# S5's small matmuls and the sums of squares with left operands of 64 columns, and S5's gate placed later among the output projection

## The chip, the cores and the metric

The kernel runs on one core of one Trainium2 chip. The metric is the time of one execution on the device, in microseconds (us); lower is better. The core has a matrix engine (PE; its weight loads are shown as a row of their own, PEld), a vector engine (DVE), an activation engine (ACT), a general engine (POOL), and a queue engine (SP) which here issues nearly all transfers between the chip's main memory and the on-chip memory. The engines run side by side. Each works through its own list of instructions in the order in which the program gives them, and an instruction waits until what it needs has been produced. So a matmul late in PE's list never overtakes one that waits ahead of it.

A matmul on PE has a left operand, which is loaded into the array first (LDWEIGHTS, the PEld row), and a right operand that is streamed through it. A float32 operand takes two passes: one matmul in the source is then two LDWEIGHTS and two MATMUL in the trace. Operands of the type F32R take one.

## The reference

Two decoder layers over 512 positions of width 1024. Layer 0 mixes by two paths whose outputs are concatenated and projected; layer 1 mixes by a short convolution. Each layer ends with a gated feed-forward network (FFN). The part that the change touches is layer 0's S5 path, and the normalisations' sums of squares.

```
y = rmsnorm(h, mix_norm_g[0])
p = y @ ev_w_in                                  # 256 columns for S5, 1536 for gMLP
# S5: 16 groups of 16 channels, each drives 64 complex states
x_re, x_im = u @ bb_re, u @ bb_im
h_re, h_im = associative_scan(a, x)              # h[t] = a * h[t-1] + x[t]
a_out = gelu(h_re @ c_re - h_im @ c_im + d_skip * u)
a_out = a_out * sigmoid(a_out @ w_glu + b_glu)   # the gate (GLU)
# gMLP: gelu, rmsnorm of v, 128x128 causal mixing of positions, 6 heads
b_out = u * gate
h = h + concat(a_out, b_out) @ ev_w_out          # the output projection
h = h + conv_ffn(rmsnorm(h, ...))
...
return rmsnorm(h, final_norm_g)
```

## The kernel before, in words

Channels lie on the 128 partitions, the 512 positions along a row, so the residual `h` is eight tiles of 128x512. Every large matmul is done in three F32R matmuls (`mms`, lines 135 to 137): high part by high part, low part by high part, high part by low part. A step's weight is loaded into a `raw` tile, split into a high part `whi` by ACT (line 111) and a low part `wlo` by DVE (line 112); each of these has three buffers, so a load waits until the split three steps earlier is done, and a split waits until the matmuls three steps earlier have read their weights.

The program is a list of steps, one per weight tile. In layer 0 they are: eight steps `eva` of the input projection (`first`), four `evv` (`v_unit`, the second half of gMLP's v), five `evu` (`head`, gMLP's u; the last three also do the mixing `spatial`, whose outputs are the tiles `ab0` to `ab5`), eight `evo` (the output projection of gMLP's part, one of eight output tiles `pe` each), and two `evos` (the output projection of S5's part, four output tiles `pes` each). For the first three `evo` steps the last two of the six inner tiles are put off until all three have done the first four. After `evos` each finished tile of `h` is prepared for the FFN (`xprep`: high part `xhf` on ACT, low part `xlf` on DVE, squares on ACT and POOL), and the FFN's matmuls (`pf`) follow.

S5 is not a step. It is a Python generator, `s5_all`, that writes its instructions between the steps: it yields an estimated cost in us after each piece, and ahead of each step `bg` lets it go on for as many us as a table gives (`BG_A` for the `eva` steps, `BG_B` from there on; its last entry holds for all later steps). Its pieces, in order:

- parameters, and tables of powers, on DVE;
- `s5_near` (line 619): the near part of the kernel, 16 matmuls into `pnr`, an addition on POOL, two transposes into `pnt`, then a way through main memory (`dnr`) into the tile `tm`;
- `s5_state`: matmuls into `pbu`, a scan on DVE, and four tiles `xo` (two for each c, the real and the imaginary part);
- `s5_out` (line 650): for each of two halves i, 8 groups of three matmuls into `py`, then a gelu into `yt`, and a way through main memory: one store into `dy` and eight loads into `yg`, all on the SP queue;
- `s5_glu` (line 668): for each half i two matmuls of 512 columns into `pgl` (one with `yg0`, one with `yg1`), sigmoid on ACT into `sg`, a product on DVE into `so`, and the split into `as0` and `as1`, which the `evos` steps read.

The matmuls into `pbu` already have left operands of 64 columns, and write the upper and the lower 64 partitions in turn:

```
r = slice(64 * (g % 2), 64 * (g % 2) + 64)
PE.matmul(pv[c][r, j * NC:(j + 1) * NC], lhsT=win[c][:, j, r], rhs=us[:, g, :],
          start=True, stop=True)
```

`sum_mm` (line 196) adds the squares over the partitions: a matmul with the squares as left operand and two columns as right operand, per 128 positions. It is used three times: once for the first normalisation (into `pstm`) and twice for the last (into `pstfin`, once per half of the positions). The other normalisations use `wide_stats` instead.

The code fixes which instructions exist and their order of need. Their place in each engine's list is then decided when the program is built: a scheduler that simulates the engines orders them, so pieces of neighbouring steps can be interleaved.

Of the kernel before, what the change touches and what calls it, by code (L numbers as in the profile page):

```python
# [16 lines left out]
P = 128  # L17
# [6 lines left out]
LAG = (2, 3)  # L24
LATE = 2
SP0 = 3
BG_A = (0.0, 2.0, 2.0, 3.0, 4.0, 4.5, 4.5, 4.5)
BG_B = (1.5, 3.0, 3.0, 3.0, 3.4, 3.4, 3.0, 2.5, 2.5, 2.5)
L = 8
NC = T // L  # L30
# [21 lines left out]
def trunk(ctx: ExitStack, tc: tile.TileContext, x, pra, prb, eva, evu, evv, evo, evos, bmat, bmatz, cmat, wglu,  # L52
          wst, bs, odi, odo, up, dn, out):
    nc = tc.nc
    V, G, S, PE = nc.vector, nc.gpsimd, nc.scalar, nc.tensor
# [8 lines left out]
    def pt(name):  # L64
        return ps.tile([P, T], F32, tag="mm", name=name)

    def gt(name, dt=F32R):
        return gp.tile([P, T], dt, tag="g", name=name)
# [10 lines left out]
    onesd = cp.tile([P, 2], F32, name="onesd")  # L79
# [35 lines left out]
    def advance(upto, bg=None):  # L115
        while state["load"] < min(upto + 3, len(steps)):
            load(state["load"])
            state["load"] += 1
        while state["split"] < min(upto + 2, len(steps)):
            split(state["split"])  # L120
            state["split"] += 1

    def run_steps(n0, n1, bg=None, cost=None):

        for i in range(n0, n1):
            advance(i)
            if bg is not None:
                bg(cost(i - n0))
            steps[i][1](*state["spl"][i])
# [65 lines left out]

    def sum_mm(pst, a, n, first, last):
        for i in range(n):
            PE.matmul(pst[:, 2 * i:2 * i + 2], lhsT=a[:, i * P:(i + 1) * P], rhs=onesd,
                      start=first and i == 0, stop=last and i == n - 1)

    def inv_rms(pst, tag, n):
        m = cp.tile([P, 8], F32, tag="m", name=f"m{tag}", bufs=2)[:, :n]
# [43 lines left out]
    env = {}  # L246
# [3 lines left out]
    def bychunk(ap):  # L250

        return ap.rearrange("p (c s) -> p s c", s=L)

    def cvw(ap):
        return ap.rearrange("p (s c) -> p s c", s=L)
# [31 lines left out]
    us = sp.tile([P, NG, NC], F32, name="us")  # L287
# [53 lines left out]
    def head_out(n, pu):  # L341
        ug = sp.tile([P, T], F32, tag="ug", name=f"ug{n}", bufs=SP0 + 1)
        V.tensor_tensor(out=ug, in0=pu, in1=env["rs"], op=ALU.mult)
        S.activation(ug, ug, AF.Gelu_apprx_tanh)
        ugs[n] = ug

    def head(n):
        def f(hi, lo):
            pu = pt(f"phu{n}")
            mms(pu, hi, lo, xs, range(KD), 0, KD - 1)  # L350
            head_out(n, pu)
            if n >= SP0:
                spatial(n - SP0)
            if n == 5:
                for m in range(6 - SP0, 6):
                    spatial(m)
# [19 lines left out]
    bmz = sp.tile([P, 2, 8, 32], F32, name="bmz")  # L376
# [6 lines left out]
    def ttt(o, a, b, op):  # L383
        V.tensor_tensor(out=o, in0=a, in1=b, op=op)  # L384
# [41 lines left out]
    ca = [sp.tile([P, 8, L + 1, 16], F32, name=f"ca{c}") for c in range(2)]  # L426
    win = [sp.tile([P, 8, P], F32, name=f"win{c}") for c in range(2)]
    tm = sp.tile([P, NG, P], F32, name="tm")
# [192 lines left out]
    def s5_near():  # L621

        dd = gt("dd", F32)[:16, :256].rearrange("p (g r) -> p g r", r=16)
        G.tensor_tensor(out=dd, in0=ident[0:16, 0:16].unsqueeze(1).to_broadcast([16, NG, 16]),
                        in1=pa[0:16, A_D:A_D + NG].unsqueeze(2).to_broadcast([16, NG, 16]), op=ALU.mult)
        nr = gt("nr", F32)[:, :256]
        pn = pt("pnr")
        for j in range(8):
            for c in range(2):
                PE.matmul(pn[:, 32 * j:32 * j + 32], lhsT=ca[c][:, j, 0:L, :].rearrange("p n r -> p (n r)"),  # L630
                          rhs=bmz[:, c, j, :], start=(c == 0), stop=(c == 1))
        S.copy(nr, pn[:, :256])
        o = nr[0:16, :].rearrange("p (g r) -> p g r", r=16)
        G.tensor_tensor(out=o, in0=o, in1=dd, op=ALU.add)
        pn2 = pt("pnt")
        for i in range(2):
            PE.transpose(pn2[:, i * P:(i + 1) * P], nr[:, i * P:(i + 1) * P], ident)
        nt = gt("nt", F32)[:, :256]
        S.copy(nt, pn2[:, :256])
        for i in range(2):  # L640
            nc.sync.dma_start(dnr[i * P:(i + 1) * P, :], nt[:, i * P:(i + 1) * P])
        for q in range(L):
            w = 16 * (q + 1)
            nc.sync.dma_start(tm[16 * q:16 * q + 16, :, P - w:],
                              dnr.rearrange("(g h) c -> h g c", h=16)[:, :, :w])
        wgl.append(gt("wglu", F32).rearrange("p (k c) -> p k c", c=256))
        nc.sync.dma_start(wgl[0], wglu)
        yield 1.0

    def s5_out():  # L650
        for i in range(2):
            yg[i] = gt(f"yg{i}", F32)
            py = pt(f"py{i}")
            for g in range(8):
                o = py[:, g * NC:(g + 1) * NC]
                for c in range(2):
                    PE.matmul(o, lhsT=ca[c][:, 4 * i + g // 2, 1:, :].rearrange("p n r -> p (n r)"),
                              rhs=env[f"xo{c}"][i][:, g * NC:(g + 1) * NC], start=(c == 0), stop=False)
                PE.matmul(o, lhsT=tm[:, 8 * i + g, :], rhs=us[:, 8 * i + g, :], start=False, stop=True)
            yt = gt(f"yt{i}", F32)  # L660
            S.activation(yt, py, AF.Gelu_apprx_tanh)
            nc.sync.dma_start(dy[i], yt)
            for g in range(8):
                nc.sync.dma_start(cvw(yg[i][16 * g:16 * g + 16, :]),
                                  dy[i].rearrange("(s h) (g c) -> g h s c", h=16, c=NC)[g])
        yield 2.0

    def s5_glu():
        for i in range(2):
            pgl = pt(f"pgl{i}")  # L670
            for k in range(2):
                PE.matmul(pgl, lhsT=wgl[0][:, k, i * P:(i + 1) * P], rhs=yg[k], start=(k == 0), stop=(k == 1))
            sg = sp.tile([P, T], F32, tag="vsq", name=f"sg{i}")
            S.activation(sg, pgl, AF.Sigmoid, bias=pa[:, A_BG + i:A_BG + i + 1])
            so = sp.tile([P, T], F32, tag="sc", name=f"so{i}", bufs=2)
            ttt(bychunk(so), cvw(sg), cvw(yg[i]), ALU.mult)
            yk[i] = split_to(so, f"as{i}")
            yield 2.0

    def s5_all():  # L680
        yield from s5_params()
        yield from s5_in_w()
        yield from s5_c()
        yield from s5_in_w_turn()
        yield from s5_out_w()
        yield from s5_near()
        yield from rot_table()
        yield from s5_state()
        yield from s5_out()
        yield from s5_glu()  # L690

    class Bg:
        def __init__(self, gen):
# [194 lines left out]
    eA = len(steps)  # L888
    steps += [((evv[kk], 768), v_unit(kk)) for kk in range(4)]
    steps += [((evu[n], 1024), head(n + 1)) for n in range(5)]  # L890
    e1 = len(steps)
    ev = out_group(yk, 2, KD, lambda d, p: add_back(d, p, None), "e", 3, LATE)
    steps += [((evo[d], 768), ev(d)) for d in range(KD)]
    e15 = len(steps)
# [15 lines left out]
    bg = Bg(s5_all())  # L910
# [26 lines left out]
    for k in range(KD):  # L937
        advance(k)
        for q in (2 * k + 2, 2 * k + 3):
            if q < KD:  # L940
                take_x(q)
        bg(BG_A[k])
        first(k, *state["spl"][k])
# [8 lines left out]
    for n in range(6):  # L952
        G.affine_select(out=wt[:, n, :], in_=wt[:, n, :], pattern=[[1, P]], compare_op=ALU.is_ge,
                        fill=0.0, base=0, channel_multiplier=-1)
    run_steps(eA, e15, bg, lambda i: BG_B[min(i, len(BG_B) - 1)])
    bg(1e9)
    run_steps(e15, e2)
    p1.close()
    fp["p"] = ctx.enter_context(tc.tile_pool(name="fp", bufs=2))
# [92 lines left out]
```

## Time and profile before

| | us |
|---|---|
| median of 3 runs | 1074.59 |
| lowest and highest | 1073.94, 1075.92 |
| the profiled execution's own time | 1073.31 |
| its span, first to last instruction | 1071.5 |
| PE busy in that span | 1053.0 |
| DVE, ACT, POOL busy | 670.8, 420.4, 135.4 |

The profile is one execution. In a timeline row the first number is the start in us from the beginning of the span, the second the length of the row's work; x64 at the end means 64 instructions merged in that row. Matmuls are pipelined: a MATMUL of 390 ns is followed by the next one after some 230 ns, so what a matmul costs is the distance from start to start, not its own length. A note in brackets at the end of a row is the idle time of that engine just ahead of it and what ended it. The granted TensorE clock is full (1.00) in all the stretches used here.

### The profile page before, as it was taken

How to read it: one execution, taken by the hardware profiler on the slowest of the kernel's cores; microseconds unless marked ns; L12 is line 12 of the kernel's file. 1: busy time of each engine (PE TensorE's matmuls, PEld its weight loads, DVE VectorE, ACT ScalarE, POOL GpSimd, SP SyncE). 2: the span in 40 equal slices, each digit the busy share in tenths (PEclk: the TensorE clock that was granted, in tenths of full speed). 3: DMA queues.
4: the chain of work that ended last, by engine and by line, in shares of the span. 5: the costliest groups of instructions: out<-in, count | busy, mean ns of one | idle time of the engine just before them, and what ended most of it. 6: DMA issues, size and time to landing. Idle time of an engine off the chain costs nothing.

```text
span 1071.5 us, 12604 instructions
## 1 busy us (share of the span) xinstructions
PE 1053.0 (98%) x4928; PEld 882.3 (82%) x4928; DVE 670.8 (63%) x937; ACT 420.4 (39%) x565; POOL 135.4 (13%) x121
## 2 busy tenths in 40 slices
PE   7999999999999999999999999999999999999996
PEld 6998788888888888888888888888888888888885
DVE  7968369866346663566585564678645664666544
ACT  6444245544134431344522232444423432444343
POOL 3010012201000100011311110302000100010012
PEclk9999999999999999999999999999999999999998
DMA  7451232323323333222323331423232233232322
GB/s 257 128 134 60 89 114 83 100 97 98 99 98 98 98 99 98 99 79 79 120 97 98 98 98 59 138 80 101 76 119 98 89 89 118 98 99 84 84 70 79
DMA packets 39979, 107.17 MB, mean 100 GB/s; under 512 B 10224, under 2 KB 11248, under 8 KB 39920
## 3 DMA queue, kind: packets, MB, share of 16 engines
q1 hardware_dynamic: 39920, 106.37, 31.5%
q8 instruction: 38, 0.62, 0.2%
q14 instruction: 21, 0.17, 0.1%
HBM read 103.08 MB, written 3.28 MB: 99 GB/s over the span
## 4 chain that ended last, share of the span: by engine, by line
PE 98%; DVE 1%; DMA 0%; ACT 0%; issue 0%; SPq 0%; POOL 0%; DVEq 0%; ACTq 0%; POOLq 0%
PE pf L137 15%; PE pf L136 15%; PE pf L135 15%; PE pd L137 11%; PE pd L136 11%; PE pd L135 11%; PE po L137 1%; PE po L135 1%; PE po L136 1%; PE pv L279 1%; PE pv L281 1%; PE pv L280 1%; PE pe L135 1%; PE pe L137 1%; PE pe L136 1%; PE phu L135 1%
## 5 line engine op out<-in xcount | busy, mean ns | idle before, releaser
L111 ACT CAST whi<-raw 128x1024 fp32r<-128x1024 f32 (+3 forms) x204 | 198.7, 977 | 450.0 <-PE pd L136 200.7
L112 DVE TENSOR_TENSOR wlo<-raw,whi 128x1024 fp32r<-128x1024 f32 (+3 forms) x204 | 246.7, 1210 | 49.7 <-ACT whi L111 49.2
L137 PE MATMUL pf<-xhf,wlo 128*128 128x512 f32 x704 | 273.9, 389 | 0.0
L136 PE MATMUL pf<-xlf,whi 128*128 128x512 f32 x704 | 273.6, 389 | 0.0
L135 PE MATMUL pf<-xhf,whi 128*128 128x512 f32 x704 | 273.5, 389 | 0.0
L136 PEld LDWEIGHTS pf<-xlf,whi 128*128 128x128 f32 x704 | 132.1, 188 | 27.8 <-DVE xlf L145 0.2
L135 PEld LDWEIGHTS pf<-xhf,whi 128*128 128x128 f32 x704 | 132.1, 188 | 27.5
L137 PEld LDWEIGHTS pf<-xhf,wlo 128*128 128x128 f32 x704 | 132.1, 188 | 27.2
L384 DVE TENSOR_TENSOR hs<-pf,rsf 128x512 f32<-128x512 f32 x88 | 60.5, 691 | 127.0 <-PE pf L137 126.9
L775 POOL TENSOR_TENSOR cv<-cv,cv 128x512 f32<-128x512 f32 x44 | 58.5, 1328 | 571.5 <-DVE cv L748 529.4
L384 DVE TENSOR_TENSOR hall<-hall,pd 128x512 f32<-128x512 f32 x48 | 32.9, 687 | 101.5 <-PE pd L137 101.5
L137 PE MATMUL pd<-xhm,wlo 128*128 128x512 f32 x192 | 74.7, 389 | 0.0
L136 PE MATMUL pd<-xlm,whi 128*128 128x512 f32 x192 | 74.7, 389 | 0.0
L135 PE MATMUL pd<-xhm,whi 128*128 128x512 f32 x192 | 74.7, 389 | 0.0
L746 ACT ACTIVATE cv<-hs,pb 128x512 f32<-128x512 f32 x88 | 71.4, 816 | 7.4 <-DVE hs L384 6.0
L748 DVE SCALAR_TENSOR_TENSOR cv<-hs,pb,cv 128x512 f32<-128x512 f32 x88 | 66.1, 751 | 2.8
L747 DVE SCALAR_TENSOR_TENSOR cv<-hs,pb,cv 128x512 f32<-128x512 f32 x88 | 67.5, 770 | 0.0
L772 ACT ACTIVATE cv<-cv 128x512 f32<-128x512 f32 x44 | 27.8, 632 | 81.5 <-DVE cv L748 81.4
L135 PEld LDWEIGHTS pd<-xhm,whi 128*128 128x128 f32 x192 | 36.0, 188 | 7.6
L136 PEld LDWEIGHTS pd<-xlm,whi 128*128 128x128 f32 x192 | 36.0, 188 | 7.5
L137 PEld LDWEIGHTS pd<-xhm,wlo 128*128 128x128 f32 x192 | 36.0, 188 | 7.4
L157 POOL TENSOR_TENSOR acc<-acc,sqf 128x512 f32<-128x512 f32 x14 | 23.2, 1654 | 55.3 <-ACT sqf L156 55.0
(577 smaller groups left out, 1586.1 us busy)
## 6 DMA issues: line engine op xcount, KB each, us to landing
raw<-up SPq DMA_DIRECT2D x88, 512.0 KB, 3.3
raw<-dn SPq DMA_DIRECT2D x32, 384.0 KB, 3.1
raw<-odi SPq DMA_DIRECT2D x24, 512.0 KB, 3.3
raw<-dn SPq DMA_DIRECT2D x16, 512.0 KB, 3.5
raw<-odo SPq DMA_DIRECT2D x8, 512.0 KB, 3.3
raw<-evo SPq DMA_DIRECT2D x8, 384.0 KB, 3.1
raw<-eva SPq DMA_DIRECT2D x7, 384.0 KB, 6.7
raw<-evu SPq DMA_DIRECT2D x5, 512.0 KB, 3.4
```

Of the source, the lines that this page charges most:

```text
L111: S.copy(hi[:, c], r[:, c])
L112: V.tensor_tensor(out=lo[:, c], in0=r[:, c], in1=hi[:, c].bitcast(F32), op=ALU.subtract)
L135: PE.matmul(dst, lhsT=hi[:, c], rhs=xh, start=(k == first), stop=False)
L136: PE.matmul(dst, lhsT=hi[:, c], rhs=xl, start=False, stop=False)
L137: PE.matmul(dst, lhsT=lo[:, c], rhs=xh, start=False, stop=(k == last))
L157: eng.tensor_tensor(out=acc, in0=acc, in1=sq, op=ALU.add)
L384: V.tensor_tensor(out=o, in0=a, in1=b, op=op)
L746: S.activation(o, src[:, 2:T + 2], AF.Identity, scale=w2, bias=b)
L747: V.scalar_tensor_tensor(out=o, in0=src[:, 1:T + 1], scalar=w1, in1=o, op0=ALU.mult, op1=ALU.add)
L748: V.scalar_tensor_tensor(out=o, in0=src[:, 0:T], scalar=w0, in1=o, op0=ALU.mult, op1=ALU.add)
L772: S.activation(c, c, AF.Silu)
L775: G.tensor_tensor(out=c, in0=c, in1=fp["gate"], op=ALU.mult)
```

## The change

Three things. The matmuls of `sum_mm`, `s5_near` and `s5_out` are written as two each, with 64 columns of the left operand, which write partitions 0 to 63 and 64 to 127 of the same output. `s5_near` yields 2.0 once more, ahead of its transposes. And `s5_glu` leaves `s5_all`: what is left of S5 is finished ahead of the sixth `evo` step (`GLU = 5`), and the two halves of the gate are written ahead of the sixth and seventh `evo` step.

```
+GLU = 5
...
     def sum_mm(pst, a, n, first, last):
         for i in range(n):
-            PE.matmul(pst[:, 2 * i:2 * i + 2], lhsT=a[:, i * P:(i + 1) * P], rhs=onesd,
-                      start=first and i == 0, stop=last and i == n - 1)
+            for e in (0, 64):
+                PE.matmul(pst[e:e + 64, 2 * i:2 * i + 2], lhsT=a[:, i * P + e:i * P + e + 64], rhs=onesd,
+                          start=first and i == 0, stop=last and i == n - 1)
...
             for c in range(2):
-                PE.matmul(pn[:, 32 * j:32 * j + 32], lhsT=ca[c][:, j, 0:L, :].rearrange("p n r -> p (n r)"),
-                          rhs=bmz[:, c, j, :], start=(c == 0), stop=(c == 1))
+                for e in range(2):
+                    PE.matmul(pn[64 * e:64 * e + 64, 32 * j:32 * j + 32],
+                              lhsT=ca[c][:, j, 4 * e:4 * e + 4, :].rearrange("p n r -> p (n r)"),
+                              rhs=bmz[:, c, j, :], start=(c == 0), stop=(c == 1))
         S.copy(nr, pn[:, :256])
         o = nr[0:16, :].rearrange("p (g r) -> p g r", r=16)
         G.tensor_tensor(out=o, in0=o, in1=dd, op=ALU.add)
+        yield 2.0
         pn2 = pt("pnt")
...
             for g in range(8):
-                o = py[:, g * NC:(g + 1) * NC]
+                o = [py[64 * e:64 * e + 64, g * NC:(g + 1) * NC] for e in range(2)]
                 for c in range(2):
-                    PE.matmul(o, lhsT=ca[c][:, 4 * i + g // 2, 1:, :].rearrange("p n r -> p (n r)"),
-                              rhs=env[f"xo{c}"][i][:, g * NC:(g + 1) * NC], start=(c == 0), stop=False)
-                PE.matmul(o, lhsT=tm[:, 8 * i + g, :], rhs=us[:, 8 * i + g, :], start=False, stop=True)
+                    for e in range(2):
+                        PE.matmul(o[e], lhsT=ca[c][:, 4 * i + g // 2, 1 + 4 * e:5 + 4 * e, :]
+                                  .rearrange("p n r -> p (n r)"),
+                                  rhs=env[f"xo{c}"][i][:, g * NC:(g + 1) * NC], start=(c == 0), stop=False)
+                for e in range(2):
+                    PE.matmul(o[e], lhsT=tm[:, 8 * i + g, 64 * e:64 * e + 64], rhs=us[:, 8 * i + g, :],
+                              start=False, stop=True)
...
         yield from s5_out()
-        yield from s5_glu()
...
-    run_steps(eA, e15, bg, lambda i: BG_B[min(i, len(BG_B) - 1)])
+    run_steps(eA, e1 + GLU, bg, lambda i: BG_B[min(i, len(BG_B) - 1)])
     bg(1e9)
+    glu = Bg(s5_glu())
+    run_steps(e1 + GLU, e15, glu, lambda i: 2.0)
+    glu(1e9)
     run_steps(e15, e2)
```

The code moves more than the diff tells, since the scheduler places what follows. On PE, at the seam between gMLP's mixing (`pg`) and the output projection (`pe`), before:

```order
L362 MATMUL pg5_1170<-wt_104,vg2_97 128x128
L362 MATMUL pg5_1170<-wt_104,vg3_98 128x128
L657 MATMUL py0_1189<-xo0_0_1040,ca0_125 128x64
L657 MATMUL py0_1189<-xo1_0_1096,ca1_126 128x64
L659 MATMUL py0_1189<-us_99,tm_129 128x64
```

and in the changed kernel (xo0_0 is c = 0 and i = 0; whi17, 18, 19 are the weights of the first three `evo` steps):

```order
L364 MATMUL pg5_1184<-wt_104,vg3_98 128x128
L136 MATMUL pe_0_1212<-ab0h_1050,whi17_1104 128x512
L137 MATMUL pe_0_1212<-ab0l_1051,whi17_1104 128x512
L138 MATMUL pe_0_1212<-ab0h_1050,wlo17_1105 128x512
L136 MATMUL pe_0_1212<-ab1h_1098,whi17_1104 128x512
L137 MATMUL pe_0_1212<-ab1l_1099,whi17_1104 128x512
L138 MATMUL pe_0_1212<-ab1h_1098,wlo17_1105 128x512
L663 MATMUL py0_1232<-xo0_0_1110,ca0_125 64x64 x2
L663 MATMUL py1_1293<-xo0_1_1111,ca0_125 64x64 x2
L136 MATMUL pe_1_1353<-ab0h_1050,whi18_1198 128x512
```

All 48 matmuls into `py` stood right behind `pg` before; now the first three `evo` steps (54 matmuls) come first, only two pairs of `py` stand among them, and the other 46 pairs follow behind the third step.

Again on PE, the gate (`pgl`). Before, the product with `yg0` stood behind the first `evo` step and that with `yg1` behind the third:

```order
L137 MATMUL pe_0_1262<-ab5h_1178,wlo17_1093 128x512
L672 MATMUL pgl0_1281<-yg0_1188,wglu_806 128x512
L672 MATMUL pgl1_1292<-yg0_1188,wglu_806 128x512
L135 MATMUL pe_1_1303<-ab0h_1028,whi18_1184 128x512
...
L672 MATMUL pgl0_1281<-yg1_1225,wglu_806 128x512
L672 MATMUL pgl1_1292<-yg1_1225,wglu_806 128x512
L135 MATMUL pe_3_1362<-ab0h_1028,whi20_1318 128x512
```

In the changed kernel they stand behind the fifth step, behind the sixth, and after a third of the seventh:

```order
L138 MATMUL pe_4_1438<-ab5h_1192,wlo21_1409 128x512
L681 MATMUL pgl0_1464<-yg0_1231,wglu_891 128x512
L136 MATMUL pe_5_1475<-ab0h_1050,whi22_1434 128x512
...
L138 MATMUL pe_5_1475<-ab5h_1192,wlo22_1435 128x512
L681 MATMUL pgl1_1501<-yg0_1231,wglu_891 128x512
...
L138 MATMUL pe_6_1512<-ab1h_1098,wlo23_1461 128x512
L681 MATMUL pgl0_1464<-yg1_1292,wglu_891 128x512
L681 MATMUL pgl1_1501<-yg1_1292,wglu_891 128x512
L136 MATMUL pe_6_1512<-ab2h_1156,whi23_1460 128x512
```

So 36 matmuls of `pe` stand between the last of `py` and the first of `pgl` (18 before, counted from the end of the whole `py` block), and 30 between the last of `pgl` and the first of `pes` (90 before).

On the SP queue, the way of S5's output through main memory (`dy`, `yg`), before:

```order
L97 DMA raw22_1356<-evo 128x768
L662 DMA dy0_102<-yt0_1214 128x512
L664 DMA yg0_1188<-dy0_102 16x8x64 x8
L662 DMA dy1_103<-yt1_1251 128x512
L664 DMA yg1_1225<-dy1_103 16x8x64 x8
L97 DMA raw23_1382<-evo 128x768
```

and now:

```order
L98 DMA raw22_1406<-evo 128x768
L98 DMA raw23_1432<-evo 128x768
L98 DMA raw24_1458<-evo 128x768
L98 DMA raw25_1495<-evos 128x1024
L671 DMA dy0_102<-yt0_1281 128x512
L673 DMA yg0_1231<-dy0_102 16x8x64 x8
L671 DMA dy1_103<-yt1_1342 128x512
L673 DMA yg1_1292<-dy1_103 16x8x64 x8
L98 DMA raw26_1532<-evos 128x1024
```

Three more weight loads stand ahead of `dy0`; the numbers of the buffers count the steps, so the load of `raw25` reuses the buffer of `raw22`, the weight of the sixth `evo` step.

## The prediction

> **What bounds the kernel now.** I read the page's first lines, then the chain that ended last, then the list of PE's waits.
>
> ```profile
> span 1071.5 us, 12604 instructions
> PE 1053.0 (98%) x4928; PEld 882.3 (82%) x4928; DVE 670.8 (63%) x937; ACT 420.4 (39%) x565; POOL 135.4 (13%) x121
> PE 98%; DVE 1%; DMA 0%; ACT 0%; issue 0%; SPq 0%; POOL 0%; DVEq 0%; ACTq 0%; POOLq 0%
> ...
> PE pu L270 <- ACT whi L111: 7.7, 1, 7.7
> PE pbcfin L212 <- DVE rtfin L168: 2.5, 1, 2.5
> PE pstfin L198 <- POOL acc L834: 1.6, 1, 1.6
> PE pgl L672 <- PE pe L137: 0.3, 1, 0.3
> ```
>
> The reader is to see that PE is the bound from end to end: 98% of the chain, and only four waits, of which the first is the start and two are the very end. Between 8 us and 1058 us PE waits once, at the gate, for 0.3 us by this list. So a microsecond of PE's issue time saved in the middle is a microsecond of the kernel, as long as nothing that PE reads comes late instead.
>
> **What a small matmul costs.** A busy PE says nothing of speed, so I took distances from start to start in the timeline: from the first small matmul of a group to the first ordinary one behind it.
>
> ```profile
> 73.23 0.39 PE L137 MATMUL phu<-xhm,wlo 128*128 128x512 f32 x1
> 73.55 2.08 PE L580 MATMUL pbu<-us,win 128*64 128x64 f32 x64
> 75.56 0.50 PE L135 MATMUL phu<-xhm,whi 128*128 128x512 f32 x1
> 75.89 0.39 PE L136 MATMUL phu<-xlm,whi 128*128 128x512 f32 x1
> 76.13 0.40 PE L137 MATMUL phu<-xhm,wlo 128*128 128x512 f32 x1
> ...
> 60.04 3.65 PE L630 MATMUL pnr<-bmz,ca 128*128 128x32 f32 x32
> 63.53 0.42 PE L279 MATMUL pv<-whi,xhm 128*128 128x384 f32 x1
> ...
> 26.36 0.95 PE L198 MATMUL pstm<-onesd,acc 128*128 128x2 f32 x8
> 27.17 1.03 PE L198 MATMUL pstm<-onesd,sqm 128*128 128x2 f32 x8
> 28.06 0.48 PE L270 MATMUL pu<-xhm,whi 128*128 128x512 f32 x1
> ```
>
> With left operands of 128 columns, `pnr` takes 63.53 - 60.04 = 3.49 us for 32 instructions, 109 ns each; `pstm` 1.70 us for 16, 106 ns each. The width of the right operand (32 or 2) hardly matters. With 64 columns, the `pbu` group takes 75.56 - 73.55 = 2.01 us for 64, **31.4 ns** each. Two halves thus cost 63 ns where a whole costs 106 to 109: loads into the two column halves overlap. Going in costs 73.55 - 73.23 = 0.32 us where an ordinary step is 76.13 - 75.89 = 0.24, so about 0.09 more; coming out 0.33 instead of 0.24, another 0.09.
>
> The pattern that the change writes is that of `pbu`: 128 rows deep, 64 columns, 64 wide at `py`, halves in turn. This is the main evidence for it.
>
> ```profile
> L657 PE MATMUL py<-xo,ca x64: 222/275/275, 102.8 to 113.2; 128*128 128x64 f32 x64
> L659 PE MATMUL py<-us,tm x32: 275/275/275, 103.2 to 113.4; 128*128 128x64 f32 x32
> ...
> 102.84 0.56 PE L657 MATMUL py<-xo,ca 128*128 128x64 f32 x4
> 113.48 0.48 PE L135 MATMUL pe<-ab0h,whi 128*128 128x512 f32 x1
> ```
>
> **The sum, part by part.** Each group doubles its count at 31.4 ns:
>
> - `py`: 96 instructions in 113.48 - 102.84 = 10.64 us become 192, 6.03 us. They now stand in two blocks, so I add 0.30 for going in twice and out once more. Saved: 4.31.
> - `pnr`: 3.49 becomes 64 x 31.4 ns = 2.01, plus 0.09. Saved: 1.39.
> - `pstm`: 1.70 becomes 32 x 31.4 ns = 1.00, plus 0.09. Saved: 0.61. That a right operand of 2 or 32 columns is as quick as 64 no row shows; above, width did not matter, so I take 31.4. From the other side the halves could cost as much as the wholes together (55 ns), which would save nothing here.
>
> ```profile
> 1048.82 0.50 PE L198 MATMUL pstfin<-onesd,acc 128*128 128x2 f32 x4
> ...
> 1049.38 0.50 PE L198 MATMUL pstfin<-onesd,sqf 128*128 128x2 f32 x4
> ...
> 1049.94 0.28 PE L137 MATMUL pl<-g_18h,wlo 128*128 128x256 f32 x1
> ...
> 1060.52 0.61 PE L198 MATMUL pstfin<-onesd,acc 128*128 128x2 f32 x4 [1.59 <-POOL acc L834]
> 1060.99 0.59 PE L198 MATMUL pstfin<-onesd,sqf 128*128 128x2 f32 x4
> ```
>
> - `pstfin`, first half: 1.12 us from 1048.82 to 1049.94 with two matmuls of `pl` in it, some 0.2 too much for 16 instructions in one block. Saved: 0.2.
> - `pstfin`, second half, in the tail where DVE waits for it: 8 instructions at 108 ns become 16 at 31.4. Saved: 0.26 after 0.1 for going in.
>
> ```profile
> 117.46 0.39 PE L137 MATMUL pe<-ab5h,wlo 128*128 128x512 f32 x1
> 118.18 0.67 PE L672 MATMUL pgl<-yg,wglu 128*128 128x512 f32 x1 [0.34 <-PE pe L137]
> ...
> 110.51 0.33 SPq L662 DMA_DIRECT2D dy<-yt  x1
> 112.66 3.65 SPq L664 DMA_DIRECT2D yg<-dy  x8
> 116.41 0.37 SPq L662 DMA_DIRECT2D dy<-yt  x1
> 118.75 3.63 SPq L664 DMA_DIRECT2D yg<-dy  x8
> ...
> yg<-dy SPq DMA_DIRECT2D x16, 32.0 KB, 1.9
> ```
>
> - The gate's wait. The first `pgl` starts at 118.18 where 117.46 + 0.24 = 117.70 was due: 0.48 lost. The releaser named is PE itself, long done; it is the loads of `yg0`, the last issued by 116.31, 1.9 us to landing, 118.2. Saved: 0.48, if `yg` is in time at its new place.
>
> Sum: 4.31 + 1.39 + 0.61 + 0.2 + 0.26 + 0.48 = **7.25 us** of PE time.
>
> **What could be late next.** Four joints lose cover, and PE's whole list stands behind each.
>
> ```profile
> 105.42 0.69 DVE L336 TENSOR_TENSOR ab2l<-gg,ab2h 128x512 fp32r<-128x512 f32 x1
> ...
> 128.19 1.88 PE L672 MATMUL pgl<-yg,wglu 128*128 128x512 f32 x4
> 130.13 0.40 PE L136 MATMUL pe<-ab0l,whi 128*128 128x512 f32 x1
> ...
> 133.01 0.69 DVE L336 TENSOR_TENSOR as0l<-so,as0h 128x512 fp32r<-128x512 f32 x1 [0.74 <-ACT as0h L335]
> 135.43 0.69 DVE L336 TENSOR_TENSOR as1l<-so,as1h 128x512 fp32r<-128x512 f32 x1 [0.69 <-ACT as1h L335]
> ...
> 167.74 2.44 DVE L145 SCALAR_TENSOR_TENSOR xlf<-hall,pb,xhf 128x512 fp32r<-128x512 f32 x2
> ```
>
> (1) `ab2` to `ab5`: the `py` block hid them before; `pe` now starts at about 100.9 (102.84 less 0.61 and 1.39). Adding up DVE's new list in its own durations (`xo` with c = 1 now stands behind `ab5l`) I get `ab2l` at about 105.5; PE wants it some 22 matmuls on, near 106.1. It holds, by 0.6. The other `ab` have more.
> (2) `yg`: from the store's issue to landing took 118.2 - 110.5 = 7.7 us for `yg0`, and `yg1` came 6.1 later. `py0` now ends 23 pairs, 2.9 us, ahead of `py1`, and behind that stand 36 matmuls (8.3 us) to the first `pgl`, and 24 more and two `pgl` (7 us) to that with `yg1`. Both are in time by some 2.5 us.
> (3) `as`: the gate's last matmuls were over at 130.13 - 0.24 = 129.9, `as0l` ended at 133.7 and `as1l` at 136.1, 3.8 and 6.2 us later. The 30 matmuls left are 6.9 us, and the scheduler put the parts with `as0` of three outputs ahead of those with `as1`. In time by 2 to 3.
> (4) `xlf`: the first `pes` output is complete ten matmuls later within its step (2.3 us), so DVE's chain of additions and `xlf`, which ended at 170.2 with PE close behind, starts later too; the new order gives PE four other matmuls (0.9 us) first. This is the thinnest. I allow 0.3 us, between 0 and 1.
>
> So 7.25 - 0.3, say **7.0 us**. On the profiled execution's own 1073.31 (span 1071.5 and 1.8 around it) that is 1066.3. The median shown, 1074.59, stands 1.3 above that execution and all three runs are above it; on it, 1067.6. I forecast between the two, **1067.0**, and for this case alone 1065 to 1069.
>
> **A rule weighed.** The pair of rows at 73.23 and 75.56 shows some 0.2 us for going into and out of the 64-column form. The Trainium skill, "TensorEngine Tiling (Array Packing)", section Key Properties, says that a change of tiling mode drains TensorE; that speaks against a change with more such groups. Draining at both ends of all six new blocks, at 390 - 240 = 150 ns a time by the ordinary row, would take 1.8 us, against the 0.8 in my sum: 1 us less gain, within the range.
>
> **The rivals.**
> *A, a joint is late.* One of the four costs 2 to 4 us, most likely `xlf` or `yg`. Against it speaks the slack worked out above; for it, that my sums over DVE's list can be off by half a microsecond at each joint, and that the scheduler placed the new order by its own estimates. Time: 1069 to 1071.
> *B, the halves don't pair.* If new halves are issued at 53 to 56 ns, half of today's 106 to 111, 320 instructions take what 160 do now and only the gate's wait is won: about 1073.5. Against it stands `pbu` at 31.4; for it, that no row shows 64 columns with several matmuls accumulating, or so narrow a right operand. The Trainium skill, "TensorE: Matmul & The Clock Gate", section "Wait — 56ns, not 53.3ns?", gives some 62 ns per matmul where instructions are decoded by firmware; that would make it 320 x 62 ns = 19.8 us instead of 17.6, an estimate of about 1075 by that page, but the 31.4 ns of `pbu` contradicts it here.
> *C, slower: `dy0` held up on the SP queue.* Three more weight loads stand ahead of it, and one such load has waited long for its buffer:
>
> ```profile
> SPq L97 <- DVE wlo L112: 865.7, 187, 13.9
> ```
>
> A wait of 13.9 us right ahead of `dy0` would, less 2.5 us of slack, stop PE for 11.4 us at `pgl`: 7.25 gained and 11.4 lost is +4, near 1078. It is slower by over 0.2% from a hold of 12 us on. Against it: the last load ahead of `dy0` reuses the buffer of the sixth step, whose split waits only for the third step's matmuls, and these end ahead of the `py` block. So the hold should end about when `yt0` is ready.
>
> **How the numbers follow.** Forecast 0.75, A 0.13, B 0.07, C 0.05. The measurement tells about 0.2% (2 us) from no change; the forecast and A are faster by more, B is the same, C slower. So faster 0.88, same 0.07, slower 0.05. The range 1064.8 to 1071.0 holds nearly all of the forecast and most of A, and leaves out B and C.
>
> **What would show it.** In the changed profile: `py` near 6 us in all, `pnr` near 2.0, `pstm` near 1.0; no idle time ahead of `pgl`; PE's waits unchanged in number but for the gate's. I am wrong if a small matmul takes over 40 ns, if PE waits for `as`, `ab`, `xlf` or `yg`, or if the FFN's matmuls go at another pace than before, since no part of the sum touches them.

## The result and the profile after

The changed kernel takes **1066.91 us** (median of 6 runs, 1065.37 to 1068.12) where the kernel before takes 1074.33 beside it (6 runs, 1071.79 to 1075.92): a ratio of 0.9932, with a 95% interval of 0.9919 to 0.9945, so 5.9 to 8.7 us less. The forecast was 1067.0. The profiled execution took 1065.93 (span 1064.2).

The first lines of the profile's page of the changed kernel:

```profile
span 1064.2 us, 12925 instructions
PE 1046.4 (98%) x5088; PEld 874.1 (82%) x5088; DVE 668.0 (63%) x937; ACT 419.6 (39%) x565; POOL 135.1 (13%) x121
```

And the list of PE's waits (total, times, longest):

```profile
PE pu L272 <- ACT whi L112: 6.3, 1, 6.3
PE pbcfin L214 <- DVE rtfin L169: 2.5, 1, 2.5
PE pstfin L200 <- POOL acc L842: 1.6, 1, 1.6
PE pgl L681 <- DMA yg<-dy: 1.0, 1, 1.0
```

PE is still the bound, with 160 records more and 6.6 us less of busy time. The wait ahead of `pgl` did not go, as the prediction had it: it grew to 1.0 us, and now its releaser is named, the loads of `yg`.

The three groups of small products, and the gate, in the timeline of the changed kernel (start, length, engine, line, operation, tiles):

```profile
24.92 0.63 PE L200 MATMUL pstm<-onesd,acc 128*64 128x2 f32 x16
25.41 0.61 PE L200 MATMUL pstm<-onesd,sqm 128*64 128x2 f32 x16
25.95 0.50 PE L272 MATMUL pu<-xhm,whi 128*128 128x512 f32 x1
...
58.15 2.06 PE L633 MATMUL pnr<-bmz,ca 128*64 128x32 f32 x64
60.14 0.44 PE L281 MATMUL pv<-whi,xhm 128*128 128x384 f32 x1
...
112.12 0.39 PE L138 MATMUL pe<-ab5h,wlo 128*128 128x512 f32 x1
112.44 0.34 PE L663 MATMUL py<-xo,ca 128*64 128x64 f32 x4
...
117.96 0.50 PE L136 MATMUL pe<-ab0h,whi 128*128 128x512 f32 x1
...
126.02 0.39 PE L138 MATMUL pe<-ab5h,wlo 128*128 128x512 f32 x1
127.39 1.10 PE L681 MATMUL pgl<-yg,wglu 128*128 128x512 f32 x2 [0.98 <-DMA yg<-dy]
```

From start to start, `pnr` now takes 60.14 - 58.15 = 1.99 us for 64 records, 31.1 ns each, and `pstm` 1.03 us for 32, 32 ns. The second block of `py` has 184 of its 192 records in 117.96 - 112.44 = 5.52 us, 30.0 ns. Where `pe` ends at 126.02, `pgl` was due at 126.25 and started at 127.39, 1.14 late.

Why `yg0` is late stands on SP's queue, of the changed kernel:

```profile
113.83 1.79 SPq L98 DMA_DIRECT2D raw<-evo  x2
116.16 0.33 SPq L98 DMA_DIRECT2D raw<-evos  x1
116.54 0.42 SPq L671 DMA_DIRECT2D dy<-yt  x1
121.89 3.64 SPq L673 DMA_DIRECT2D yg<-dy  x8
```

The store `dy0` was issued at 116.54, and the first load of `yg0`, which waits for it, at 121.89: 5.35 us, where the rows of before have 112.66 - 110.51 = 2.15. Three weight loads (384, 384 and 512 KB) were issued in the 2.7 us ahead of the store.

**What the code changed, apart from chance.** The first wait of PE, at the start, is 1.4 us shorter than in the profile of before, ahead of any changed instruction. To leave that out I use one stretch in every profile: from the first `pu` matmul behind `pstm` to the statistics at the end of layer 0, found with the view of the tile `pstm`:

```profile
L184 PE MATMUL pstm<-acm1h,onesr x1: 404/404/404, 525.4 to 525.4; 128*128 128x512 f32 x1
```

```profile
L183 PE MATMUL pstm<-acm1h,onesr x1: 404/404/404, 532.3 to 532.3; 128*128 128x512 f32 x1
```

The first row is of the changed kernel, the second of the kernel before. The stretch is 525.4 - 25.95 = 499.4 us after and 532.3 - 28.06 = 504.2 before: 4.8 less. Worked out the same way for the kernels of the experiments (`pstm` and `pstfin` lie outside it):

| kernel | median, us | ratio to the runs of before beside it (95%) | the stretch, us |
|---|---|---|---|
| before | 1074.33 | | 504.2 |
| changed | 1066.91 | 0.9932 (0.9919 to 0.9945) | 499.4 |
| a8, changed, run again | 1066.88 | 0.9943 (0.9928 to 0.9958) | 499.0 |
| e1, split alone | 1072.78 | 0.9990 (0.9981 to 0.9999) | 505.4 |
| e2, move alone | 1074.18 | 1.0002 (0.9990 to 1.0014) | 505.3 |
| e3, halves not in turn | 1072.83 | 0.9990 (0.9981 to 1.0000) | 505.2 |
| e4, store on ACT's queue | 1065.72 | 0.9925 (0.9910 to 0.9940) | 498.3 |
| e5, quarters | 1071.94 | 0.9981 (0.9971 to 0.9990) | 505.2 |
| e6, as e4, `pg` in halves | 1066.66 | 0.9934 (0.9920 to 0.9947) | 499.5 |
| e7, no second step | 1064.41 | 0.9915 (0.9902 to 0.9927) | 497.5 |
| f1, as e7, quarters in the small groups | 1063.89 | 0.9907 (0.9893 to 0.9921) | 497.0 |
| f2, as f1, `py` too | 1067.36 | 0.9939 (0.9926 to 0.9952) | 500.5 |
| f3, as e7, gate at step two | 1066.65 | 0.9931 (0.9918 to 0.9945) | 498.7 |
| f4, before with `pnr` twice | 1080.44 | 1.0056 (1.0039 to 1.0072) | |

### The profile page after: what moved, and what is told of

Same layout as the page of the kernel before. It is cut to its first block, busy times and chain, and to the rows that moved or that the text cites. A ratio compares the mean times of both kernels' runs of the same rounds, so it can differ in the third digit from the quotient of the medians.

```text
span 1064.2 us, 12925 instructions
## 1 busy us (share of the span) xinstructions
PE 1046.4 (98%) x5088; PEld 874.1 (82%) x5088; DVE 668.0 (63%) x937; ACT 419.6 (39%) x565; POOL 135.1 (13%) x121
## 4 chain that ended last, share of the span: by engine, by line
PE 96%; DMA 1%; DVE 1%; SPq 0%; issue 0%; ACT 0%; POOL 0%; DVEq 0%; ACTq 0%; POOLq 0%
PE pf L137 15%; PE pf L136 15%; PE pf L138 15%; PE pd L138 11%; PE pd L136 11%; PE pd L137 11%; PE po L138 1%; PE po L136 1%; PE po L137 1%; PE pv L281 1%; PE pv L283 1%; PE pv L282 1%; PE phu L136 1%; PE phu L137 1%; PE phu L138 1%; PE pe L136 1%
```

## The experiments

### e1 and e2: the two parts of the change alone

e1 is the changed kernel with the gate part back behind `s5_out` and without the added step:

```
-    run_steps(eA, e1 + GLU, bg, lambda i: BG_B[min(i, len(BG_B) - 1)])
+    run_steps(eA, e15, bg, lambda i: BG_B[min(i, len(BG_B) - 1)])
     bg(1e9)
-    glu = Bg(s5_glu())
-    run_steps(e1 + GLU, e15, glu, lambda i: 2.0)
-    glu(1e9)
...
         yield from s5_out()
+        yield from s5_glu()
```

> The three groups of small products and the sums of squares split in halves; the gate part and the steps stay where they were in the kernel before. Theory 1 (the whole gain is PE's issue time in the split groups, and the move of the gate part only keeps yg in time): py in one block takes about 6.1 us, pnr 2.0, pstm 1.0, as in the changed kernel; but py now ends 4.5 us earlier, and yg0 lands only 7.7 us after dy0's issue, so the first pgl waits about 2.6 us instead of 0.5. Time 1074.3 - 7.2 + 0.5 + 2.1 = about 1069.7, 4.6 us under the kernel before. Theory 2 (the move itself carries a good part of the gain): less than 3 us gained, 1071.5 or more, with no long wait ahead of pgl. Theory 3 (the move is worth nothing or costs): 1067 or less, no long wait ahead of pgl.

1072.78 us: 1.5 less than before, where 4.6 were expected. `py` took 5.75 us in one block, `pnr` 1.99 and `pstm` 1.03, so the split paid what it should. The wait ate it. The timeline of e1:

```profile
109.78 0.39 PE L138 MATMUL pe<-ab5h,wlo 128*128 128x512 f32 x1
115.16 3.75 PE L680 MATMUL pgl<-yg,wglu 128*128 128x512 f32 x4 [4.99 <-DMA yg<-dy]
117.92 1.42 PE L136 MATMUL pe<-ab0h,whi 128*128 128x512 f32 x1
...
126.00 1.88 PE L680 MATMUL pgl<-yg,wglu 128*128 128x512 f32 x4
127.32 0.79 PE L137 MATMUL pe<-ab5l,whi 128*128 128x512 f32 x1
```

Windows of e1 behind the wait (length, busy time of PE, PEld, DVE, ACT and POOL, then the granted clock, the DMA share and GB/s):

```profile
115.16:117.92 2.76, 2.76 (x4) 1.21 (x5) 0.00 (x0) 0.00 (x0) 0.20 (x1) 0.50 0.53 166
117.92:121.01 3.09, 3.09 (x9) 2.10 (x8) 0.00 (x0) 0.00 (x0) 0.00 (x0) 0.55 0.24 51
121.01:126.00 4.99, 4.99 (x23) 4.13 (x22) 0.00 (x0) 0.00 (x0) 0.00 (x0) 1.00 0.03 7
```

PE waits 5.0 us for `yg0`, twice what was expected: `dy0` was issued only at 107.62, since the splits of `ab4` and `ab5` stood ahead of the activation on ACT. And behind the wait the clock is at 0.50 up to 120.6, some 5.5 us. The first four `pgl` records take 117.92 - 115.16 = 2.76 us; the later four, at full clock, 127.32 - 126.00 = 1.32. The six `pe` behind the first group take 121.01 - 117.92 = 3.09 us where six behind the later group take 1.8. The slow clock so costs 1.4 + 1.3 = 2.7 us on top of the wait. The profiled run is no exception: the mean granted clock is 0.993 or 0.994 in all 12 runs of e1, and 0.995 or 0.996 in the six of the table for the changed kernel.

e2 is the kernel before with the gate part and the step moved, its operands whole.

> The gate part and the steps moved as in the changed kernel; all left operands stay whole (128 columns). Theory 1: only the gate's wait of 0.5 us can be won, and yg has 2.6 us more time than in the changed kernel since the last py group takes 5.3 us longer: about 1073.9, within 0.1% of the kernel before, and no wait ahead of pgl. Theory 2 (the move carries a good part of the gain): 3 us or more gained, 1071.3 or less.

1074.18 us, ratio 1.0002: no difference, and no wait ahead of `pgl`, as theory 1 had it. Together: the split alone gives 1.5 us, the move alone nothing, both 7.4. The gain is PE's time in the split groups; the move is what lets the kernel keep it.

### e3: the halves not in turn

The same 320 half matmuls, but all left halves of a group first, then all right ones (`py` shown; `pnr` and the sums alike):

```
-            for g in range(8):
-                o = [py[64 * e:64 * e + 64, g * NC:(g + 1) * NC] for e in range(2)]
+            for e in range(2):
+                for g in range(8):
+                    o = py[64 * e:64 * e + 64, g * NC:(g + 1) * NC]
```

> As the changed kernel, with the same 320 half matmuls and the same placement, but in each group all of the left half come first and then all of the right half, so that neighbours lie in the same half. Theory 1 (halves are quick because the loads of one half overlap the other half's work): they go at 53 to 56 ns, half of a whole one; the 304 ahead of the last stage cost 304 x (55 - 31) ns = 7.3 us more than in the changed kernel, about 1074, and py takes about 10.5 us. Rival (a 64-column operand is simply quicker to load and to issue): the pace stays near 31 ns, py near 6 us, time 1067.

1072.83 us, 5.9 over the changed kernel. In the timeline of e3:

```profile
58.81 3.59 PE L633 MATMUL pnr<-bmz,ca 128*64 128x32 f32 x62
62.33 0.45 PE L282 MATMUL pv<-wlo,xhm 128*128 128x384 f32 x1
```

3.52 us for 62 records, 56.8 ns each, and the second block of `py` 10.57 us for 188, 56.2 ns. So a 64-column left operand that follows one of the same half costs half a whole one (109 ns), and the 31 ns need neighbours in different halves. The single records of the traces show how: in `pnr` of the changed kernel the loads of the two halves start 6 to 7 ns apart, and a new pair every 58 ns; in e3 one load starts every 58 ns. The two halves are worked on side by side. Of the 7.3 us expected 5.9 came: with `py` 5 us longer `yg` is in time, and e3 has no wait ahead of `pgl` (1.1 us less).

### e4: is it the queue?

```
-            nc.sync.dma_start(dy[i], yt)
+            nc.scalar.dma_start(dy[i], yt)
```

> As the changed kernel, but the two stores of yt go out on ACT's DMA queue instead of SP's, right behind the activation that makes yt. Theory 1 (yg0 came late because its store stood on SP's queue behind three weight loads of 1.28 MB, 5.35 us from its issue to the first load of yg where it took 2.15 before): the store lands about 3 us earlier, the wait ahead of pgl goes from 1.1 us to nothing, 1065.8, 1.1 under the changed kernel. Rival (the store shares the DMA engines with the weight loads whatever its queue): the first load of yg is still issued about 5 us behind the store, the wait stays at 1 us, 1066.9.

The time is that expected, 1065.72, but not for the reason given, and its interval overlaps that of the changed kernel. ACT's queue in the timeline of e4:

```profile
117.90 0.34 ACTq L671 DMA_DIRECT2D dy<-yt  x1
```

And SP's:

```profile
122.55 8.11 SPq L673 DMA_DIRECT2D yg<-dy  x16
```

On a queue of its own the store still takes 4.65 us until `yg` may be loaded (changed kernel: 5.35, in its second profile 4.8). The loads under way on the same DMA engines delay it, as the rival said. Two of them were issued ahead of it here and the third 0.15 us behind it. While the store runs, the DMA engines' busy share is 0.91 in e4 and 0.78 in the changed kernel, where the store takes long, and 0.32 in the kernel before, e1 and e7, where it takes 2.15 us. The window from the store to the first load of `yg`, of e4 and then of e7 (described below):

```profile
117.90:122.55 4.65, 4.65 (x82) 4.13 (x78) 0.12 (x1) 0.60 (x1) 0.00 (x0) 1.00 0.91 281
107.79:109.94 2.15, 2.15 (x11) 1.77 (x10) 0.20 (x1) 0.47 (x1) 0.00 (x0) 1.00 0.32 122
```

What the queue gave is that the store is issued 0.02 us behind its activation instead of 0.55. The wait was 0.26 us.

### e7 and a8: the added step

e7 is the changed kernel without `yield 2.0` in `s5_near`; a8 is the changed kernel again, on the same chip.

> As the changed kernel without the added step of two units in the projection's background work: py stands in one block directly behind the last pg, one step earlier, and the gate part stays at its new place. Theory 1 (what the new place of the gate part must do is to leave yg its 8 us, and any earlier place of py only adds to that): no wait ahead of pgl, 1.1 us less than the changed kernel, about 1065.8. Rival (the later place of py is needed, since xo or ab come late for PE or ACT without it): a new wait of PE of 1 us or more around py or ab, 1067 or more.

> The changed kernel again, unaltered, on the same chip as the three before, with a second profile: 1066.9 by the earlier runs. Theory 1: the first wait of PE (start-up), which stood at 6.3 us in its first profile and at 7.7 in that of the kernel before, varies from run to run between these without any change in code, and the wait ahead of pgl of about 1 us is there again. Rival: the start-up wait is 6.3 us again in the changed kernel, so that part of the 7.3 us comes from the start.

a8: 1066.88 us (1066.06 to 1069.78). Its start-up wait is 7.0 us, and in all profiles of the study it lies between 6.0 and 7.9 whatever the code, so that part of the first pair of profiles was chance. The wait ahead of `pgl` is there again, 0.7.

e7: 1064.41 us (1064.07 to 1064.85), 2.5 under a8, and its stretch is 1.5 shorter (PE's first wait, which lies outside it, is 6.0 us in e7's profile and 7.0 in a8's). SP's queue in the timeline of e7:

```profile
107.79 0.33 SPq L670 DMA_DIRECT2D dy<-yt  x1
109.94 4.59 SPq L672 DMA_DIRECT2D yg<-dy  x8
```

And PE's rows where `pgl` starts in it:

```profile
122.65 0.39 PE L137 MATMUL pe<-ab0l,whi 128*128 128x512 f32 x1
122.88 1.02 PE L680 MATMUL pgl<-yg,wglu 128*128 128x512 f32 x2
```

With `py` one step earlier the store has no weight loads beside it (2.15 us, the old price), and 74 matmuls cover what follows: no wait. Of the 1.5 us, 0.9 is a8's wait (`pgl` at 128.38, due at 127.51), 0.2 the second block of `py`, and 0.2 lies behind the first `pf` (the `xlf` of joint 4). So the step that the change added does harm here; the new place of the gate part alone is enough. Against e1, which differs from e7 only in the place of the gate, the stretch is 505.4 - 497.5 = 7.9 us shorter: 5.15 of wait and 2.7 of slow clock.

### f3: the gate at another place

e7 with `GLU = 2`, that is 36 matmuls between `py` and the first `pgl` instead of 74.

> As e7, with the gate part from the projection's step two on instead of five: 36 matmuls of the projection between py and the first pgl instead of 74. yg0 landed at 115 us in e7; pgl is due at 105.95 + 36 x 0.23 = 114.2, so PE waits about 1 us. Theory 1 (the gate part's place matters only through the wait for yg, and a wait of 1 us costs no more than itself): 1064.4 + 1.0 = 1065.4, granted clock 1.00 behind the wait. Rival (the late place of the gate part has another gain or cost of its own, or a short wait also lowers the clock): below 1064 or above 1066.5.

1066.65 us; the stretch is 1.2 us longer than in e7. From the timeline of f3:

```profile
115.41 0.39 PE L138 MATMUL pe<-ab5h,wlo 128*128 128x512 f32 x1
116.77 1.10 PE L680 MATMUL pgl<-yg,wglu 128*128 128x512 f32 x2 [0.97 <-DMA yg<-dy]
```

116.77 - 115.64 = 1.13 us late, as the slack gave it, and the clock is at 1.00 behind it. The place acts through the wait alone. The median is 0.15 us above 1066.5, from where the rival was to hold; the trace decides for theory 1.

### e5, f1 and f2: quarters

e5 splits all three groups of the changed kernel in four of 32 columns, in turn.

> As the changed kernel, with the left operands of py, pnr and the sums of squares split in four of 32 columns, the quarters in turn, instead of two of 64. The trace records two matmuls for each of these products, so ahead of the last stage 288 records become 576. Theory 1 (31 ns is a floor per instruction, whatever its width): the quarters go at 31 ns, 288 x 31 ns = 8.9 us more than in the changed kernel, 1075.8. Theory 2 (31 ns is half of the 56 ns that the load of 64 columns takes, since two halves overlap; narrower is quicker in proportion): 14 to 16 ns, the same total, 1067. In between: the Trainium skill, TensorE: Matmul & The Clock Gate, section Wait - 56ns, not 53.3ns?, puts the floor from start to start at about 25 ns; that would be 576 x 25 - 288 x 31 ns = 5.5 us more, 1072.4, an estimate by that page.

1071.94 us, and neither theory holds. From the timeline of e5:

```profile
58.44 1.30 PE L633 MATMUL pnr<-bmz,ca 128*32 128x32 f32 x128
59.66 0.44 PE L281 MATMUL pv<-whi,xhm 128*128 128x384 f32 x1
...
114.69 0.29 PE L667 MATMUL py<-us,tm 128*32 128x64 f32 x8
116.59 0.43 PE L663 MATMUL py<-xo,ca 128*32 128x64 f32 x16 [1.60 <-issue]
...
118.29 0.29 PE L663 MATMUL py<-xo,ca 128*32 128x64 f32 x8
122.23 0.44 PE L663 MATMUL py<-xo,ca 128*32 128x64 f32 x8 [3.65 <-issue]
```

`pnr` takes 1.22 us for 128 records, **9.5 ns each**: 31 ns was no floor, and the 25 ns that the Trainium skill, "TensorE: Matmul & The Clock Gate", section "Wait — 56ns, not 53.3ns?", gives as the least distance from start to start does not hold for quarters. `py`, with twice the columns on the right, goes at 14 ns, but twice PE stands still inside it, waiting for nothing that the profile shows, and the clock is at 0.50 from 121.0, inside the second standstill, to 127.9. That, not the pace, costs the 5 us.

f1 takes e7 and puts quarters in `pnr` and the sums only; f2 in `py` too.

> As e7 (no second step), with quarters of 32 columns in pnr and in the sums of squares only; py stays in halves. By e5's trace 128 records of pnr took 1.22 us and 64 of the sums 0.65 us, against 1.99 and 1.03 in halves: 0.77 + 0.38 us less, and some 0.2 in the two pstfin. Theory 1 (e5 lost its time in py alone): 1064.4 - 1.3 = 1063.1, and no wait for issue. Rival (quarters anywhere starve PE of instructions): a wait marked issue of over 1 us, 1065 or more.

> As f1, with py in quarters too: 384 records in one block, at another place than in e5, with no weight load under way beside the block but the one issued just ahead of it. Theory 1 (PE runs dry of instructions in a long block at 14 ns each, wherever it stands, since instructions come by DMA and cannot keep up): waits marked issue inside py again, 2 us or more in all, 1065 or more; at over 2.5 us in one piece the clock drops behind it as well. Theory 2 (in e5 the fetch of instructions was late only because three weight loads ran at the same time): no wait in py, which takes 5.4 instead of 5.75 us, 1062.7.

f1: 1063.89 us, no wait for issue. The stretch is 0.5 shorter than e7's and `pstm` 0.4, together less than expected; by their times e7 and f1, which were not run side by side, can't be told apart. f2: 1067.36, 3.5 more. PE's waits in f2:

```profile
PE py L662 <- issue: 1.7, 1, 1.7
...
PE py L666 <- issue: 1.4, 1, 1.4
```

The standstill is back at another place, with one weight load under way at the start of the block. Runs of 64 (`pstm`) and 128 short records (`pnr`) pass; those of 368 (e5) and 384 (f2) don't. In both kernels exactly 128 records, 256 instructions with their loads, lie between the two standstills, and in the first one of f2 (101.8 to 103.4) the DMA share is 0.00, so weight loads can't be what holds PE up there, and theory 2 is out. That PE's list of instructions is then empty, and is filled up in portions of 256, is theory 1's reading with this count; it fits both runs, but the profile doesn't show it.

### e6: more groups in halves

e4 with the products `pg` in halves too:

```
-            PE.matmul(pg[:, t * P:(t + 1) * P], lhsT=vg[t][:, n * P:(n + 1) * P],
-                      rhs=wt[:, n, :], start=True, stop=True)
+            for e in (0, 64):
+                PE.matmul(pg[e:e + 64, t * P:(t + 1) * P], lhsT=vg[t][:, n * P + e:n * P + e + 64],
+                          rhs=wt[:, n, :], start=True, stop=True)
```

> As e4 (stores of yt on ACT's queue), and the products pg of the spatial part, 48 records of 128 columns with a right operand of 128, 117 ns each, split in halves in turn as well. Theory 1 (halves overlap in load and in stream, so about 31 ns also with 128 columns on the right): 96 x 31 = 3.0 us instead of 5.6, 2.6 us less, about 1063.1. Theory 2 (31 ns is the stream of 64 columns on the right and the split gives only hidden loads; 128 columns on the right take about twice as long): 56 to 62 ns each, no gain, about 1065.7. A wait ahead of pgl of up to 1 us would have to be added to either.

1066.66 us, no gain. From the timeline of e6:

```profile
97.26 3.71 PE L365 MATMUL pg<-wt,vg 128*64 128x128 f32 x64
100.90 0.50 PE L136 MATMUL pe<-ab0h,whi 128*128 128x512 f32 x1
```

64 records in 3.64 us, 56.9 ns each: with 128 columns on the right two halves cost 114 ns, as much as a whole (109 in a8, 3.48 us for 32). Theory 2 holds: the split pays only where the right operand is narrow.

### f4: a clock that falls while PE is busy

In e2, 1.6 us were lost that no wait explains: from the start of `pnr` to the tenth `pv` behind it took 66.22 - 59.50 = 6.72 us, in the kernel before 65.17 - 60.04 = 5.13. The windows of e2 around `pnr`:

```profile
59.50:63.33 3.83, 3.83 (x34) 3.83 (x33) 2.47 (x3) 1.04 (x1) 0.00 (x0) 0.91 0.48 155
63.33:66.00 2.67, 2.67 (x9) 2.67 (x10) 0.04 (x1) 0.74 (x2) 0.72 (x1) 0.50 0.74 269
```

Finer windows put the fall at 62.6, 3.1 us into `pnr` and still inside it, and the return to 1.00 at 66.0, 3.4 us later. f4 is the kernel before with `pnr` computed twice in a row (`for j in [*range(8), *range(8)]`).

> The kernel before, with the 32 records of pnr (whole left operands, 32 columns on the right) issued twice, 64 records in one run of 7.0 us. In the profile of e2 the granted clock fell to 0.50 for some 2.5 us right behind pnr, in that of the kernel before, with the same 3.5 us of pnr, it stayed at 1.00. Theory (a run of whole, narrow matmuls counts as idle for the clock although PE issues without a gap; 3.5 us of it trips the gate in some executions only, 7 us always): granted clock near 0.5 in the second half of pnr and behind it, pv at 0.5 us for about 2.5 us, time 1074.3 + 3.5 + 1 to 3 = 1079 to 1081. Rival (the fall in e2 was a chance event that has nothing to do with pnr): clock 1.00 throughout, 1077.8.

1080.44 us, 5.9 more than before beside it, as the theory had it. Windows of f4:

```profile
60.00:62.00 2.00, 2.00 (x20) 2.00 (x19) 1.13 (x1) 0.84 (x1) 0.00 (x0) 1.00 0.34 131
62.00:64.00 2.00, 2.00 (x14) 2.00 (x13) 1.93 (x4) 0.00 (x0) 0.00 (x0) 0.63 0.41 80
64.00:67.00 3.00, 3.00 (x16) 3.00 (x16) 0.84 (x2) 0.00 (x0) 0.00 (x0) 0.50 0.53 209
```

PE is busy without a gap, and some 3 us into the run of narrow matmuls the clock falls to 0.50 all the same. The 64 records take 10.8 us instead of 7.0, and the clock is still at 0.50 at 74 us. The mean granted clock is 0.990 to 0.993 in all six runs.

## Why the prediction was right, and where it wasn't

**The bound and the price** held. PE bounds the kernel, and the halves go at 30 to 32 ns as `pbu` did. Rival B is out: e3 shows that 56 ns is the price of halves that don't alternate.

**The terms**, with what the changed kernel's rows give by the same working:

| term | forecast, us | measured, us |
|---|---|---|
| `py` | 4.31 | 4.56 (10.64 less 0.38 + 5.52 and 0.18 for going in twice) |
| `pnr` | 1.39 | 1.40 |
| `pstm` | 0.61 | 0.57 |
| `pstfin`, first half and tail | 0.2 + 0.26 | 0.2 + 0.3 |
| the gate's wait | 0.48 | **-0.66** (0.48 before, 1.14 after; a8 0.87) |
| `xlf` | -0.3 | -0.2 |
| sum | 7.0 | 6.2 |

**The term that failed is the gate's wait**, joint 2. The step reads "from the store's issue to landing took 118.2 - 110.5 = 7.7 us", and this was carried over to the new place unchanged. There it took 3.2 us longer, since three weight loads had just been issued. Rival C named these loads, but only as something that could hold the queue; that they would share the DMA engines with the store was not weighed. e4 shows that it is this and not the queue, and e7 that without them the wait is gone. With the 0.5 us for which the issue of the store stood behind the loads, 3.2 us more use up the 2.5 us of slack that the step had counted, and about the 1.1 us that `pgl` came late are left. Rival A happened in small, with 1 us instead of 2 to 4.

**The other joints** held: PE waits for no `ab` and no `as`. Of `xlf` there is no wait in the list; the time from the first `pf` to the layer's end is 0.2 longer than before in the changed kernel and in a8, and the same as before in e7. **Going in and out** of the halves costs about 0.1 us each time (112.44 - 112.12 = 0.32, less 0.23), as the forecast had it; the draining rule weighed there does not show at a price of 0.15 a side.

**The time** came out at 1066.9 in part by luck. The terms give 6.2 us, and the two profiles, counted from PE's first matmul on, (1071.5 - 7.7) - (1064.2 - 6.3) = 5.9; the medians differ by 7.4. For the rest the runs point to a term that the prediction didn't have, and could not see in a profile with the clock at 1.00: the fall of the clock in a `pnr` of whole left operands (e2, f4). Every run comes with its mean granted clock. Of the 29 runs of the kernel before beside e1 to e4, eight have 0.996 and a median of 1071.8 us, as its profile has 0.996; the other 21 have 0.993 or 0.994 and a median of 1074.8. One fall as in e2's profile, 3.4 us at half speed, takes 1.7 / 1072 = 0.0016 off the mean, about the distance between the two groups. In e2, which has the same `pnr`, 9 of 12 runs are at 0.994 or below. In e3, whose `pnr` takes as long but in halves, all 12 are at 0.996, and so are, to 0.001, the six of the changed kernel. At a like clock the change is thus worth 1071.8 - 1066.9 = 4.9 us by the medians and 5.9 by the profiles, less than the 7.0 of the sum, and a clock that falls less often adds the other 1.5 to 2.5. Two of the six runs of a8 have 0.994 all the same (1069.1 and 1069.8 us), and where the clock fell in runs without a profile is not known, so the share stays an estimate.

**What was not foreseen** is how much the move matters: without it, e1, 5 us of wait and 2.7 of slow clock take nearly all that the split brings. The prediction gave the move 0.48 us.

## What to carry to other kernels

Splitting a narrow float32 product in column halves issued in turn makes it some 1.75 times as fast (109 against 62 ns for a whole) here; it needs both the alternation (e3) and a narrow right operand: with 2 to 64 columns it paid, with 128 (e6) it did not. A faster stage shortens the cover of every transfer behind it, so count the cover again at the consumer (e1), and take a transfer's latency from the place where it will stand, with the traffic that is under way there (e4, e7). The best kernel here, f1 at 1063.89 us with e7 at 1064.41, comes from dropping one of the change's own steps.

## What the runs showed of the hardware that was not expected

- **A wait can cost more than its length.** After 1.0 us (f3, the changed kernel) and up to 1.7 us (e5, f2) of standstill the clock was 1.00; after 3.65 (e5) and 5.0 us (e1) it was 0.50, in e1 for 5.5 us. The Trainium skill, "TensorE: Matmul & The Clock Gate", section "What's actually happening", says that the clock is halved after an idle window of about 3.4 us. In e1 it falls at 113.8, 3.7 us after the last matmul ended (109.78 + 0.39), which agrees. In e5 it falls at 121.0, only some 2.4 us after `py` had stopped, and in the tail earlier still: the changed kernel's windows of the gap behind `pstfin` have a mean of 0.55 over the 2.4 us in which PE is idle, so the clock fell some 0.3 us into it, behind a wait of 1.6 us and 0.6 us of narrow matmuls (in the kernel before, 1.4 us into it). The length of the last gap alone doesn't decide; what else counts these runs don't show.

```profile
1054.20:1056.60 2.40, 0.00 (x0) 0.00 (x0) 1.94 (x12) 0.00 (x0) 0.00 (x0) 0.55 0.05 15
1056.67:1058.00 1.33, 1.19 (x4) 0.89 (x4) 0.00 (x0) 0.05 (x1) 0.00 (x0) 0.50 0.00 0
```

- **Narrow matmuls can halve the clock.** Whole left operands with 32 columns on the right (109 ns each) halve it within some 3 us though PE issues all the time (f4, e2). The 10.6 us of `py`, with 64 columns on the right (111 ns each), did not (1.00 in the windows of before), nor did the 3.5 us of e3's `pnr`, with 32 columns every 57 ns. So the length of the run alone doesn't decide; that the columns streamed per time do, 0.29 per ns against 0.58 and 0.56, fits all three, and no run here tests it further.
- **Quarters of 32 columns go at 9.5 to 14 ns**, 38 to 56 ns for a whole, and a run of 368 or 384 of them stops PE twice for 1.4 to 3.7 us (e5, f2).
